# Weight splits held back behind the gated sum and the second norm's sum in a decoder block on one core

## The chip, the cores and the metric

The kernel runs on one core of one Trainium2 chip. The metric is the time of one execution in microseconds (us), lower is better. The core's engines work side by side, each through its own row of instructions in a fixed order, and wait for one another by semaphores: TensorE (PE, matrix products), VectorE (DVE), ScalarE (ACT), GpSimd (POOL) and SyncE (SP), which here issues nearly all transfers from the main memory.

## The reference

One decoder block in float32 with 256 tokens of width 1024. Two attention branches of 8 heads run in parallel, each is multiplied with its own matrix and weighted by a sigmoid gate; the gated sum goes through `w_out`, and a gated feed-forward follows:

```python
br_a = einsum('bse,ed->bsd', o_a, w_branch_moba)
br_b = einsum('bse,ed->bsd', o_b, w_branch_fox)
merged = gates[:, :, 0] * br_a + gates[:, :, 1] * br_b
x = x + einsum('bsd,de->bse', merged, w_out)
h2 = rms_norm(x, ffn_norm_g)              # x * rsqrt(mean(x*x) + eps) * g
u, g = split(einsum('bsd,df->bsf', h2, w_ffn_up), 2)     # 2 x 2816 columns
x = x + einsum('bsf,fd->bsd', silu(conv3(g)) * u, w_ffn_down)
```

The change concerns the stretch from `br_b` to the first columns of the up-projection.

## The kernel before, in words

**Split products.** Every operand of a product is split into a high part (the value copied to PE's shortened float32 format) and a low part (value minus high part). A product is then high x high + high x low + low x high. For each half chunk of weights (128 x 1024), ACT writes the high part (line 134, `whi`) and DVE the low part (line 135, `wlo`). Such a pair is called a weight split here.

**Chunks.** The weights come in chunks of 1 MB (128 x 2048), in a fixed list: the projections, gates (`wg`), four chunks of the two branch matrices (`wb`), four of `w_out` (`wo`), then 22 of the up-projection (`wu`) with 11 of the down-projection (`wd`) among them. SP loads each into one of three buffers `raw`, and a buffer is free again when both halves in it are split. `use(chunk, half)` returns a split half and, unless `state["hold"]` is set, calls `load(upto)`, which issues the loads and splits of all halves up to a number ahead (8 from the last `wb` chunk on). Where `state["behind"]` holds a pair, the splits issued meanwhile are ordered behind these two instructions: the high part on ACT behind the first, the low part on DVE behind the second. Split halves live in six buffers `whi`/`wlo` and, from the last branch chunk on, three out of nine in `V`, `bias` and `qn`, which the attention no longer needs.

**Order.** PE's order is that of the program text. On the other engines a scheduler of the framework sets the order at build time, under the dependencies that the program gives.

**The stretch.** `branch(dh, br)` multiplies attention branch `br` for half `dh` of the columns, multiplies with the gate and, for `br == 1`, adds both branches into `gates[t][dh]` (the tile `lead`; L597 and L599 before). `turn_m(dh)` transposes this gated sum on PE (L607) and writes its high part (ACT, L611) and low part (DVE, L612) into `m2` (the tile `x2`, printed `x`). `rows_of(src, w, h, i, two)` multiplies four of the eight 128-row blocks (`h` says which four, `i` which 128 output columns): for each one pair of products, 128x512 (L641) and 128x256 (L642). The `wo` chunks go in the order (0,0), (1,0), (2,0), (0,1), (1,1), (2,1), (3,0), (3,1), with (chunk, half) in each bracket; the second turn stands within (1,0). When a chunk's columns are complete, `x1_rows(f, ...)` adds the residual (DVE, L651), writes the high and low part of the sum times the norm's gain into `hx` (the tile `pp`; ACT L654, DVE L655), squares it (ACT, L657) and adds up the squares (DVE, L661). `norm2_sum` adds the last two rows of squares (L686), splits the sum (ACT L688, DVE L689), sums over the partitions with two products with a matrix of ones (PE, L692), and computes the norm's factor `rs2` (L695 to L700), which is applied after the up-projection. The up-projection starts with chunks 0 and 1 in the order (0,0), (1,0), (0,1), (1,1), and `norm2_sum` is called within (0,1), after its first four pairs. `up_finish(f)` takes the results out of the banks (ACT L733, DVE L734), applies `rs2` (L735), the convolution and the gate, and writes the activation's parts (ACT L747, DVE L748). `down(p)` multiplies two activations with the p-th `wd` chunk (L765); the first one comes after the products of up chunk 4.

Of the kernel before, what the change touches and what calls it, by code (L numbers as in the profile page):

```python
# [8 lines left out]
F32 = mybir.dt.float32  # L9
F32R = mybir.dt.float32r  # L10
BF16 = mybir.dt.bfloat16
AF = mybir.ActivationFunctionType
ALU = mybir.AluOpType
# [4 lines left out]
P = 128  # L18
S = 256
# [23 lines left out]
def decoder_block(ctx, tc, a, out):  # L43
    nc = tc.nc
# [6 lines left out]
    def T(shape, tag, bufs=1, dt=F32):  # L51
        return sb.tile(shape, dt, tag=tag, bufs=bufs, name=tag)
# [32 lines left out]
    pos = {c: i for i, c in enumerate(chunks)}  # L85
    split = {}
    state = {"next": 0, "raw": None, "ahead": AHEAD, "hold": False, "behind": None}
# [28 lines left out]
    def load(upto):  # L116
        while state["next"] <= min(upto, 2 * len(chunks) - 1):
            i, h = divmod(state["next"], 2)
            state["next"] += 1
            if i < 2:  # L120
                lead(2 * i + h)
                continue
            c = chunks[i]
            if h == 0:
                w = 1024 if i == 2 else 2048
                src = a[c[0]]
                for j in (c[1] - (c[0] == "qkv"), *c[2:]):
                    src = src[j]
                raw = state["raw"] = T([P, 2048], "raw", RB)
                for j in range(2048 // w):  # L130
                    nc.sync.dma_start(raw[:, j * w:(j + 1) * w], src[:, j * w:(j + 1) * w])
            raw = state["raw"][:, h * 1024:(h + 1) * 1024]
            hi, lo = home(2 * i + h)
            whi = nc.scalar.activation(hi, raw, AF.Copy)  # L134
            wlo = nc.vector.tensor_tensor(lo, raw, hi.bitcast(F32), op=ALU.subtract)  # L135
            if state["behind"]:
                for i, j in zip((whi, wlo), state["behind"]):
                    if j:
                        after(i, j)
            split[c, h] = (hi, lo, whi)  # L140

    def use(c, h):
        if not state["hold"]:
            load(2 * pos[c] + h + state["ahead"])
        return split.pop((c, h))[:2]
# [60 lines left out]
    def pairs(ap):  # L206
        return ap.rearrange("p (a t) -> p t a", a=2)
# [256 lines left out]
    gates = [[lt[:, 4 * t + g, S:] for g in range(4)] for t in range(NT)]  # L464
# [26 lines left out]
    def banks():  # L491
        return [bank() for _ in range(NT)]
# [53 lines left out]
    two = [first_half(1, pair) for pair in range(2)]  # L546
# [4 lines left out]
    two = [banks() for _ in range(2)]  # L551
# [22 lines left out]
    high = values(1, (2, 3))  # L574
    for g in range(4):
        last = gate_sigmoid(g, copied if g == 3 else last_exp[0])
# [5 lines left out]
    m2 = T([P, KT, 2, 2, P], "x2", 1, F32R)  # L582
    def branch(dh, br):
        ps_ = banks()
        for hh in range(2):
            wh, wl = use(("wb", 2 * dh + br), hh)
            state["behind"] = None
            for k2 in range(2):
                k = 2 * hh + k2
                oh, ol = (x[:, 4 * br + k] for x in heads)  # L590
                rh, rl = (pairs(w[:, k2 * 512:(k2 + 1) * 512]) for w in (wh, wl))
                for i, (lhs, rhs) in enumerate(((oh, rh), (oh, rl), (ol, rh))):
                    for t in range(NT):
                        nc.tensor.matmul(ps_[t], lhs[:, t * P:(t + 1) * P], rhs, start=(k == 0 and i == 0), stop=(k == 3 and i == 2))  # L594
        for t in range(NT):
            m = gates[t][2 * br + dh]
            nc.vector.tensor_tensor(m, ps_[t], m, op=ALU.mult)  # L597
            if br == 1:
                nc.vector.tensor_tensor(gates[t][dh], gates[t][dh], m, op=ALU.add)  # L599

    def turn_m(dh):
        two = banks()
        for t in range(NT):
            for n in range(4):
                c = slice((2 * n + t) * HD, (2 * n + t + 1) * HD)
                for r, (rows, eye) in enumerate(parts):
                    nc.tensor.transpose(two[r][:, c], gates[t][dh][rows, n * P:(n + 1) * P], eye)  # L607
        for r in range(2):
            src = two[r].rearrange("p (n t c) -> p n t c", n=4, t=NT)
            high, low = (m2[:, 4 * dh:4 * dh + 4, :, l, r * HD:(r + 1) * HD] for l in range(2))  # L610
            nc.scalar.activation(high, src, AF.Copy)  # L611
            nc.vector.tensor_tensor(low, src, high.bitcast(F32), op=ALU.subtract)  # L612

    branch(0, 0)
    branch(0, 1)
    branch(1, 0)
    turn_m(0)
    state["base"], state["ahead"] = 2 * pos["wb", 3], AHEAD + 3
    branch(1, 1)


    hx = T([P, KT, 2, 2, P], "pp", 1, F32R)
# [8 lines left out]
    def wide(ps_):  # L631
        return ps_.rearrange("p (j c) -> p j c", j=2)

    def rows_of(src, w, h, i, two):
        wh, wl = w
        for k4 in range(4):
            k = 4 * h + k4
            c = slice(k4 * 256 + i * P, k4 * 256 + (i + 1) * P)
            both = src[:, k].rearrange("p a l t -> p (l t) a")
            high = src[:, k, :, 0].rearrange("p a t -> p t a")  # L640
            nc.tensor.matmul(two[i], wh[:, c], both, start=(k == 0), stop=False)  # L641
            nc.tensor.matmul(two[i][:, 0:S], wl[:, c], high, start=False, stop=(k == KT - 1))  # L642

    sums = []

    def x1_rows(f, two):
        for i in range(2):
            d = 2 * f + i
            x, g = xT[:, d], col(C_G2 + d)
            for part in (1, 0):  # L650
                nc.vector.tensor_tensor(halves(xT[:, d:d + 1]), apart(two[i][:, part * S:(part + 1) * S], 1), halves(xT[:, d:d + 1]), op=ALU.add)  # L651
            high, low = (hx[:, d, :, l] for l in range(2))
            x = x.rearrange("p (a t) -> p a t", a=2)
            nc.scalar.activation(high, x, AF.Copy, scale=g)  # L654
            nc.vector.scalar_tensor_tensor(low, x, g, high.bitcast(F32), op0=ALU.mult, op1=ALU.subtract)  # L655
        sq = T([P, 2, S], "lows", 2) if f == 0 else T([P, 2, S], "sq", 2)
        nc.scalar.activation(sq, xT[:, 2 * f:2 * f + 2], AF.Square)  # L657
        if f == 0:
            sums.append(sq)
        else:  # L660
            nc.vector.tensor_tensor(sums[0], sums[0], sq, op=ALU.add)  # L661

    tw = [banks() for _ in range(2)]
    for f in range(2):
        w = use(("wo", f), 0)
        for i in range(2):
            rows_of(m2, w, 0, i, tw[f])
            if f == 1 and i == 0:
                turn_m(1)
    tw.append(banks())  # L670
    for f, h in ((2, 0), (0, 1), (1, 1), (2, 1)):
        w = use(("wo", f), h)
        for i in range(2):
            rows_of(m2, w, h, i, tw[f])
        if h:
            x1_rows(f, tw[f])
    tw.append(banks())
    for h in range(2):
        w = use(("wo", 3), h)
        for i in range(2):  # L680
            rows_of(m2, w, h, i, tw[3])
    x1_rows(3, tw[3])

    def norm2_sum():
        ss = sums[0]
        nc.vector.tensor_tensor(ss[:, 0], ss[:, 0], ss[:, 1], op=ALU.add)  # L686
        two = T([P, 2, S], "lows", 2, F32R)
        nc.scalar.activation(two[:, 0], ss[:, 0], AF.Copy)  # L688
        nc.vector.tensor_tensor(two[:, 1], ss[:, 0], two[:, 0].bitcast(F32), op=ALU.subtract)  # L689
        o = bank()  # L690
        for l in range(2):
            nc.tensor.matmul(o[:, 0:S], ones, two[:, l], start=(l == 0), stop=(l == 1))  # L692
        w = T([P, 3, S], "s", 4)
        v, y, t = w[:, 0], w[:, 1], w[:, 2]
        nc.vector.tensor_scalar(v, o[:, 0:S], 1.0 / D, EPS, op0=ALU.mult, op1=ALU.add)  # L695
        nc.scalar.activation(t, v, AF.Ln)
        nc.scalar.activation(y, t, AF.Exp, scale=-0.5)
        nc.vector.scalar_tensor_tensor(t, v, -0.5, y, op0=ALU.mult, op1=ALU.mult)
        nc.vector.tensor_tensor(t, t, y, op=ALU.mult)
        nc.vector.scalar_tensor_tensor(rs2, t, 1.5, y, op0=ALU.add, op1=ALU.mult)  # L700
# [15 lines left out]
    def up_half(f, h, two):  # L716
        w = use(("wu", f), h)
        for i in range(2):
            rows_of(hx, w, h, i, two)
            if f == i == 0 and h == 1:  # L720
                norm2_sum()

    def up_products(f):
        two = banks()
# [77 lines left out]
    for h in range(2):  # L802
        for f in range(2):
            up_half(f, h, first[f])
    for f in range(NF):
        low = up_finish(f, first[f] if f < 2 else up_products(f))
        if f % 2 == 0 and f >= 4:
            down(f // 2 - 2)
        if TURN <= f < TURN + KT:
            turn_x(f - TURN, low)  # L810
        if f == TURN + KT:
            spread_x()
# [73 lines left out]
```

## Time and profile before

| what | value |
|---|---|
| time of the kernel, median of 3 runs | 353.95 us (353.56 to 354.65) |
| the profiled execution: its time, its span | 357.12 us, 355.3 us |
| busy: PE, weight loads, DVE, ACT | 98%, 86%, 83%, 62% of the span |
| transfers | 70.1 MB, 197 GB/s in the mean |
| mean granted TensorE clock | 0.990 |

A row of the timeline gives the start in us, the duration in us, the engine, the line and the operation, the tile written and the tiles read, and in square brackets the idle time ahead of it with what ended it. Neighbouring rows can overlap a little, since the instructions of an engine are pipelined. A row of windows gives busy microseconds of PE, weight loads (PEld), DVE, ACT and POOL in that stretch, with counts in brackets, then the granted clock, the share of the transfer engines and GB/s. A list of waits has the waiting instruction, what it waited for, the total in us, how often, and the longest.

### The profile page before, as it was taken

How to read it: one execution, taken by the hardware profiler on the slowest of the kernel's cores; microseconds unless marked ns; L12 is line 12 of the kernel's file. 1: busy time of each engine (PE TensorE's matmuls, PEld its weight loads, DVE VectorE, ACT ScalarE, POOL GpSimd, SP SyncE). 2: the span in 40 equal slices, each digit the busy share in tenths (PEclk: the TensorE clock that was granted, in tenths of full speed). 3: DMA queues.
4: the chain of work that ended last, by engine and by line, in shares of the span. 5: the costliest groups of instructions: out<-in, count | busy, mean ns of one | idle time of the engine just before them, and what ended most of it. 6: DMA issues, size and time to landing. Idle time of an engine off the chain costs nothing.

```text
span 355.3 us, 5446 instructions
## 1 busy us (share of the span) xinstructions
PE 347.5 (98%) x2047; PEld 304.1 (86%) x2047; DVE 295.9 (83%) x556; ACT 221.8 (62%) x385; POOL 1.3 (0%) x8
## 2 busy tenths in 40 slices
PE   8999999999999999999969999999999999999996
PEld 4878888888888888889959989899898989989885
DVE  5899997999689588998977997888879888887833
ACT  4868654958299394747556876556665775575420
POOL 0000000000000000000000000000000000000000
PEclk9999999999999999999978999999999999999999
DMA  7987863675612736494553555564663654546003
GB/s 275 400 331 255 289 235 129 220 259 216 225 72 70 287 118 239 129 368 171 179 220 118 194 177 222 221 209 162 238 218 138 236 218 167 223 105 237 0 2 118
DMA packets 14410, 70.10 MB, mean 197 GB/s; under 512 B 1832, under 2 KB 5040, under 8 KB 6960
## 3 DMA queue, kind: packets, MB, share of 16 engines
q1 hardware_dynamic: 13184, 68.69, 53.3%
q10 hardware_dynamic: 1200, 1.06, 0.9%
q8 instruction: 16, 0.26, 0.3%
q14 instruction: 10, 0.08, 0.1%
HBM read 67.64 MB, written 1.06 MB: 193 GB/s over the span
## 4 chain that ended last, share of the span: by engine, by line
PE 85%; DVE 6%; DMA 6%; ACT 1%; issue 1%; ACTq 0%; DVEq 0%
PE bank L246 30%; PE bank L641 21%; PE bank L765 16%; PE bank L642 10%; DMA raw<-in_wu 3%; DVE wlo L135 2%; PE bank L594 2%; PE bank L457 2%; DMA raw<-in_wo 1%; DVE lead L651 1%; PE bank L443 1%; DMA g<-in_g 1%; ACT whi L134 1%; DVE pp L655 1%; PE bank L290 1%
## 5 line engine op out<-in xcount | busy, mean ns | idle before, releaser
L135 DVE TENSOR_TENSOR wlo<-raw,whi 128x1024 fp32r<-128x1024 f32 x94 | 113.9, 1220 | 12.0 <-ACT whi L134 11.6
L134 ACT ACTIVATE whi<-raw 128x1024 fp32r<-128x1024 f32 x94 | 98.2, 1056 | 30.9 <-PE bank L641 10.7
L246 PE MATMUL bank<-whi,x 128*128 128x512 f32 x320 | 83.7, 381 | 0.2 <-DVE x L161 0.2
L641 PE MATMUL bank<-pp,whi 128*128 128x512 f32 x232 | 79.0, 391 | 0.0
L246 PEld LDWEIGHTS bank<-whi,x 128*128 128x128 f32 x320 | 59.9, 189 | 10.1 <-ACT whi L102 0.8
L642 PE MATMUL bank<-pp,wlo 128*128 128x256 f32 x232 | 64.4, 278 | 0.0
L641 PEld LDWEIGHTS bank<-pp,whi 128*128 128x128 f32 x232 | 45.1, 195 | 6.7
L246 PE MATMUL bank<-wlo,x 128*128 128x512 f32 x160 | 48.0, 381 | 0.0
L642 PEld LDWEIGHTS bank<-pp,wlo 128*128 128x128 f32 x232 | 45.6, 197 | 0.2
L246 PEld LDWEIGHTS bank<-wlo,x 128*128 128x128 f32 x160 | 29.9, 189 | 5.2 <-DVE wlo L103 0.8
L765 PE MATMUL bank<-whi,qT 128*128 128x512 f32 (+1 forms) x92 | 27.8, 370 | 0.0
L734 DVE TENSOR_TENSOR sq<-bank,lows 128x256 f32<-128x256 f32 x44 | 18.1, 416 | 10.0 <-ACT lows L733 10.0
L733 ACT ACTIVATE lows<-bank 128x256 f32<-128x256 f32 x44 | 16.1, 370 | 9.4 <-PE bank L642 8.7
L742 ACT ACTIVATE s<-s 128x256 f32<-128x256 f32 x22 | 9.1, 414 | 16.5 <-DVE s L741 16.5
L739 ACT ACTIVATE s<-sq,sm 128x256 f32<-128x256 f32 x22 | 13.1, 595 | 9.9 <-DVE sq L735 9.9
L765 PEld LDWEIGHTS bank<-whi,qT 128*128 128x128 f32 x92 | 17.2, 189 | 2.3
L641 PE MATMUL bank<-pp,bias 128*128 128x512 f32 x56 | 18.7, 382 | 0.0
L765 PE MATMUL bank<-wlo,qT 128*128 128x512 f32 (+1 forms) x46 | 17.0, 370 | 0.0
L594 PE MATMUL bank<-whi,pp 128*128 128x512 f32 x64 | 17.0, 382 | 0.0
L735 DVE TENSOR_TENSOR sq<-sq,rsB 128x512 f32<-128x512 f32 x22 | 15.2, 690 | 0.6
L642 PE MATMUL bank<-pp,bias 128*128 128x256 f32 x56 | 15.3, 273 | 0.0
L424 ACT ACTIVATE s<-s,nm 128x128 f32<-128x128 f32 (+1 forms) x32 | 14.1, 452 | 0.0
(181 smaller groups left out, 563.6 us busy)
## 6 DMA issues: line engine op xcount, KB each, us to landing
raw<-in_wu SPq DMA_DIRECT2D x22, 1024.0 KB, 4.9
raw<-in_wd SPq DMA_DIRECT2D x11, 1024.0 KB, 4.8
raw<-in_qkv SPq DMA_DIRECT2D x9, 1024.0 KB, 5.4
raw<-in_wg SPq DMA_DIRECT2D x8, 1024.0 KB, 4.9
raw<-in_wb SPq DMA_DIRECT2D x4, 1024.0 KB, 5.3
raw<-in_wo SPq DMA_DIRECT2D x4, 1024.0 KB, 4.8
lead<-in_lead SPq DMA_DIRECT2D x8, 384.0 KB, 6.0
raw<-in_qkv SPq DMA_DIRECT2D x2, 512.0 KB, 8.2
```

The source lines that it names most:

```text
L134: whi = nc.scalar.activation(hi, raw, AF.Copy)
L135: wlo = nc.vector.tensor_tensor(lo, raw, hi.bitcast(F32), op=ALU.subtract)
L246: nc.tensor.matmul(pt[t], lhs[:, k, t * P:(t + 1) * P], rhs, start=(k == 0 and i == 0), stop=(k == KT - 1 and i == 2))
L424: last_exp[:] = [nc.scalar.activation(s[:, j, c], s[:, j, c], AF.Exp, scale=-1.0, bias=nm[:, j, i:i + 1], accum_out=l[:, j, i:i + 1])]
L594: nc.tensor.matmul(ps_[t], lhs[:, t * P:(t + 1) * P], rhs, start=(k == 0 and i == 0), stop=(k == 3 and i == 2))
L641: nc.tensor.matmul(two[i], wh[:, c], both, start=(k == 0), stop=False)
L642: nc.tensor.matmul(two[i][:, 0:S], wl[:, c], high, start=False, stop=(k == KT - 1))
L733: nc.scalar.activation(lows[:, i:i + 1].rearrange("p b (a t) -> p b a t", a=2), apart(two[i][:, S:2 * S], 1), AF.Copy)
L734: nc.vector.tensor_tensor(halves(ev[:, i:i + 1]), apart(two[i][:, 0:S], 1), halves(lows[:, i:i + 1]), op=ALU.add)
L735: nc.vector.tensor_tensor(ev, ev, rs2[:, None, :].to_broadcast([P, 2, S]), op=ALU.mult)
L739: nc.scalar.activation(cv, g, AF.Identity, scale=col(C_CW + 2 * NF + f), bias=col(C_CB + f))
L765: nc.tensor.matmul(o, lhs, rhs, start=(first and i == 0), stop=(end and i == 2))
```

## The change

Three things are done. In the last branch the second half's `use` is held (`state["hold"]`), so that the splits it would have issued come after its additions, in two portions: behind the last addition (`merged`), and behind the low parts of the second turn. The second turn itself stands two pairs of products later. From chunk 3 of `wo` on, the splits are held again until the second norm's sum has been split: the sum is taken up within `x1_rows` (for chunk 3 in two half-width additions), its high and low part are written there, and the held low parts are ordered behind the last of these (`summed`). The ones products stand after the whole of (0,1) instead of after its first four pairs. Only low parts are ordered so; the high parts on ACT are not. The work itself is the same but for the shape of the additions. The names of lines move: L597 becomes L598, L599 L600, L607 L609, L611 and L612 become L613 and L614, L641 and L642 L644 and L645, L651 L654, L654 and L655 become L657 and L658, L657 L660, L692 L710, L695 L713, L733 and L734 become L751 and L752, L748 L766.

```diff
@@ branch
             state["behind"] = None
+            state["hold"] = dh == br == 1
...
             if br == 1:
-                nc.vector.tensor_tensor(gates[t][dh], gates[t][dh], m, op=ALU.add)
+                done = nc.vector.tensor_tensor(gates[t][dh], gates[t][dh], m, op=ALU.add)
+        return done if br else None
@@ turn_m
-            nc.vector.tensor_tensor(low, src, high.bitcast(F32), op=ALU.subtract)
+            last = nc.vector.tensor_tensor(low, src, high.bitcast(F32), op=ALU.subtract)
+        return last
...
-    branch(1, 1)
+    merged = branch(1, 1)
@@ rows_of
-    def rows_of(src, w, h, i, two):
+    def rows_of(src, w, h, i, two, quarters=range(4)):
...
-        for k4 in range(4):
+        for k4 in quarters:
@@ x1_rows
             sums.append(sq)
-        else:
-            nc.vector.tensor_tensor(sums[0], sums[0], sq, op=ALU.add)
+            return
+        ss = sums[0]
+        if f < 3:
+            nc.vector.tensor_tensor(ss, ss, sq, op=ALU.add)
+        if f == 2:
+            nc.vector.tensor_tensor(ss[:, 0], ss[:, 0], ss[:, 1], op=ALU.add)
+        if f == 3:
+            for i in range(2):
+                nc.vector.tensor_tensor(ss[:, 0], ss[:, 0], sq[:, i], op=ALU.add)
+            two = T([P, 2, S], "lows", 2, F32R)
+            nc.scalar.activation(two[:, 0], ss[:, 0], AF.Copy)
+            sums.append(two)
+            return nc.vector.tensor_tensor(two[:, 1], ss[:, 0], two[:, 0].bitcast(F32), op=ALU.subtract)
@@ w_out
-    for f in range(2):
-        w = use(("wo", f), 0)
-        for i in range(2):
-            rows_of(m2, w, 0, i, tw[f])
-            if f == 1 and i == 0:
-                turn_m(1)
+    w = use(("wo", 0), 0)
+    for i in range(2):
+        rows_of(m2, w, 0, i, tw[0])
+    state["hold"], state["behind"] = False, (None, merged)
+    load(2 * pos["wo", 0] + state["ahead"])
+    state["hold"] = True
+    w = use(("wo", 1), 0)
+    rows_of(m2, w, 0, 0, tw[1])
+    rows_of(m2, w, 0, 1, tw[1], range(2))
+    state["hold"], state["behind"] = False, (None, turn_m(1))
+    load(2 * pos["wo", 1] + state["ahead"])
+    state["behind"] = None
+    rows_of(m2, w, 0, 1, tw[1], range(2, 4))
...
+    state["hold"] = True
     tw.append(banks())
...
-    x1_rows(3, tw[3])
+    summed = x1_rows(3, tw[3])
@@ norm2_sum
-        ss = sums[0]
-        nc.vector.tensor_tensor(ss[:, 0], ss[:, 0], ss[:, 1], op=ALU.add)
-        two = T([P, 2, S], "lows", 2, F32R)
-        nc.scalar.activation(two[:, 0], ss[:, 0], AF.Copy)
-        nc.vector.tensor_tensor(two[:, 1], ss[:, 0], two[:, 0].bitcast(F32), op=ALU.subtract)
+        two = sums[1]
@@ up_half
-            if f == i == 0 and h == 1:
-                norm2_sum()
+        if f == 0 and h == 1:
+            norm2_sum()
@@ first up chunks
             up_half(f, h, first[f])
+            if h == f == 0:
+                state["hold"], state["behind"] = False, (None, summed)
+                load(2 * pos["wu", 0] + state["ahead"])
+                state["behind"] = None
```

What the scheduler makes of it on DVE at the second turn, first before and then now (numbers tell buffers of one name apart; `qn`, `wlo` rows are low parts of weights, `lead` the gated sum):

```order
L135 TENSOR_TENSOR qn_1682<-raw_1679,qn_1681 128x1024
L135 TENSOR_TENSOR wlo_1698<-raw_1679,whi_1697 128x1024
L597 TENSOR_TENSOR lead_78<-bank_1665,lead_78 128x512
L597 TENSOR_TENSOR lead_78<-bank_1666,lead_78 128x512
L599 TENSOR_TENSOR lead_78<-lead_78 128x512 x2
L135 TENSOR_TENSOR wlo_1728<-raw_1725,whi_1727 128x1024
```

```order
L135 TENSOR_TENSOR qn_1682<-raw_1679,qn_1681 128x1024
L598 TENSOR_TENSOR lead_78<-bank_1665,lead_78 128x512
L598 TENSOR_TENSOR lead_78<-bank_1666,lead_78 128x512
L600 TENSOR_TENSOR lead_78<-lead_78 128x512 x2
L135 TENSOR_TENSOR wlo_1738<-raw_1679,whi_1737 128x1024
L135 TENSOR_TENSOR wlo_1744<-raw_1741,whi_1743 128x1024
```

One weight split (the second half of the last `wo` chunk, out of `raw_1679`) moved from ahead of the gated sum's products and additions to behind them.

On DVE at the second norm's sum, before (from the split of up chunk 3's second half to the sum's low part):

```order
L135 TENSOR_TENSOR qn_1930<-raw_1908,qn_1929 128x1024
L651 TENSOR_TENSOR lead_78<-bank_1906,lead_78 128x256
L651 TENSOR_TENSOR lead_78<-bank_1907,lead_78 128x256
L651 TENSOR_TENSOR lead_78<-bank_1906,lead_78 128x256
L651 TENSOR_TENSOR lead_78<-bank_1907,lead_78 128x256
L135 TENSOR_TENSOR wlo_1967<-raw_1964,whi_1966 128x1024
L655 SCALAR_TENSOR_TENSOR pp_1717<-lead_78,sm_79,pp_1717 128x2x128 x2
L661 TENSOR_TENSOR lows_1847<-lows_1847,sq_1957 128x512
L135 TENSOR_TENSOR wlo_1987<-raw_1964,whi_1986 128x1024
L135 TENSOR_TENSOR wlo_1993<-raw_1990,whi_1992 128x1024
L686 TENSOR_TENSOR lows_1847<-lows_1847 128x256
L689 TENSOR_TENSOR lows_2021<-lows_1847,lows_2021 128x256
```

and now (up to the first instruction that reads the ones products, L713):

```order
L668 TENSOR_TENSOR lows_1847<-lows_1847 128x256
L654 TENSOR_TENSOR lead_78<-bank_1908,lead_78 128x256 x2
L658 SCALAR_TENSOR_TENSOR pp_1713<-lead_78,sm_79,pp_1713 128x2x128 x2
L671 TENSOR_TENSOR lows_1847<-lows_1847,sq_1949 128x256 x2
L675 TENSOR_TENSOR lows_1953<-lows_1847,lows_1953 128x256
L135 TENSOR_TENSOR bias_1978<-raw_1976,bias_1978 128x1024
L135 TENSOR_TENSOR qn_1982<-raw_1976,qn_1981 128x1024
L135 TENSOR_TENSOR wlo_1988<-raw_1985,whi_1987 128x1024
L135 TENSOR_TENSOR wlo_1992<-raw_1985,whi_1991 128x1024
L135 TENSOR_TENSOR wlo_1998<-raw_1995,whi_1997 128x1024
L713 TENSOR_SCALAR s_2036<-bank_2033 128x256
```

Five splits (`bias`, `qn` and three `wlo`: up chunks 3 and 4 and the first half of down chunk 0; the `bias` one stood a little ahead of the rows shown) moved from between and ahead of the sum's additions to behind its low part, and now stand ahead of L713.

On PE at the ones products, before and now:

```order
L641 MATMUL bank_1960<-pp_1717,whi_1747 128x512
L642 MATMUL bank_1960<-pp_1717,wlo_1748 128x256
L692 MATMUL bank_2024<-lows_2021,ones_1719 128x256 x2
L641 MATMUL bank_1961<-pp_1717,whi_1747 128x512
L642 MATMUL bank_1961<-pp_1717,wlo_1748 128x256
```

```order
L644 MATMUL bank_1957<-pp_1713,whi_1781 128x512
L645 MATMUL bank_1957<-pp_1713,wlo_1782 128x256
L710 MATMUL bank_2033<-lows_1953,ones_1715 128x256 x2
L644 MATMUL bank_1958<-pp_1713,whi_1797 128x512
L645 MATMUL bank_1958<-pp_1713,wlo_1798 128x256
```

Before, the ones products stand between the two column blocks of half (0,1), which read `whi_1747`; now they stand after both, ahead of half (1,1), which reads `whi_1797`.

## The prediction

> **What bounds the kernel now.** I read the page's busy shares and slices first, then the list of waits for TensorE (PE) alone, then the timeline around each wait it names.
>
> ```profile
> PE 347.5 (98%) x2047; PEld 304.1 (86%) x2047; DVE 295.9 (83%) x556; ACT 221.8 (62%) x385; POOL 1.3 (0%) x8
> ...
> PEclk9999999999999999999978999999999999999999
> ```
>
> PE is the bound: it is busy nearly all the time, so only what it waits for, or runs slowly through, can be won. The granted clock dips once, in slices 21 and 22 (177.7 to 195.4 us). The list of PE's waits over the whole span has four rows (in total, times, longest), two of them from the first 5 us; the other two are:
>
> ```profile
> PE bank L692 <- ACT lows L688: 3.1, 1, 3.1
> ...
> PE bank L607 <- DVE lead L599: 0.2, 1, 0.2
> ```
>
> These are two places that the change touches: the ones products (L692) and the second turn of the gated sum (L607). PE's timeline at the ones products, and the windows (us, then busy times, near the end of the row the granted clock):
>
> ```profile
> 179.03 0.40 PE L641 MATMUL bank<-pp,whi 128*128 128x512 f32 x1
> 179.27 0.27 PE L642 MATMUL bank<-pp,wlo 128*128 128x256 f32 x1
> 182.60 1.04 PE L692 MATMUL bank<-lows,ones 128*128 128x256 f32 x2 [3.06 <-ACT lows L688]
> 183.44 0.63 PE L641 MATMUL bank<-pp,whi 128*128 128x512 f32 x1
> ...
> 188.78 0.27 PE L642 MATMUL bank<-pp,wlo 128*128 128x256 f32 x1
> 188.89 0.38 PE L641 MATMUL bank<-pp,whi 128*128 128x512 f32 x1
> ```
>
> ```profile
> 181.70:181.80 0.10, 0.00 (x0) 0.00 (x0) 0.10 (x2) 0.00 (x0) 0.00 (x0) 0.61 1.17 164
> 183.44:188.56 5.12, 5.12 (x18) 4.39 (x17) 3.47 (x7) 2.21 (x5) 0.00 (x0) 0.50 0.25 104
> 188.56:193.80 5.24, 5.24 (x34) 4.82 (x33) 3.89 (x8) 3.40 (x6) 0.00 (x0) 1.00 0.58 200
> ```
>
> So the wait costs twice. PE has nothing from 179.37 (one step of 0.11 after the last start; its pipeline runs out at 179.54) to 182.60, and in that gap the clock falls to 0.50, at about 181.72 (0.61 is the mean of the tenth of a microsecond that begins at 181.70). The next 5.12 us hold eight pairs of products (0.64 each). At full clock 16 pairs take 5.24, so a pair is 0.328. Why the ones products wait is in the rows of VectorE (DVE) and ScalarE (ACT):
>
> ```profile
> 172.29 1.22 DVE L135 TENSOR_TENSOR bias<-raw,bias 128x1024 fp32r<-128x1024 f32 x1
> ...
> 174.43 1.22 DVE L135 TENSOR_TENSOR qn<-raw,qn 128x1024 fp32r<-128x1024 f32 x1
> 175.56 1.41 DVE L651 TENSOR_TENSOR lead<-bank,lead 128x256 f32<-128x256 f32 x4
> 176.89 1.21 DVE L135 TENSOR_TENSOR wlo<-raw,whi 128x1024 fp32r<-128x1024 f32 x1
> ...
> 178.81 0.68 DVE L661 TENSOR_TENSOR lows<-lows,sq 128x512 f32<-128x512 f32 x1
> 179.41 2.35 DVE L135 TENSOR_TENSOR wlo<-raw,whi 128x1024 fp32r<-128x1024 f32 x2
> 181.69 0.41 DVE L686 TENSOR_TENSOR lows<-lows 128x256 f32<-128x256 f32 x1
> 182.58 0.42 DVE L689 TENSOR_TENSOR lows<-lows 128x256 fp32r<-128x256 f32 x1 [0.48 <-ACT lows L688]
> ```
>
> ```profile
> 177.49 0.62 ACT L657 ACTIVATE sq<-lead 128x512 f32<-128x512 f32 x1
> 178.00 2.00 ACT L134 ACTIVATE whi<-raw 128x1024 fp32r<-128x1024 f32 x2
> 182.13 0.42 ACT L688 ACTIVATE lows<-lows 128x256 fp32r<-128x256 f32 x1 [2.13 <-DVE lows L686]
> ```
>
> DVE is full here, and five weight splits (bias, qn and three wlo, 1.14 us from start to start) stand among the additions that feed L689, which ends at 183.00. None of the five is needed soon: they are the up-projection's fourth and fifth chunk and the first down chunk.
>
> **The change, part by part.** *Splits behind the second norm's sum.* The five low parts now follow L675, the old L689. Taking 5 x 1.14 = 5.7 out of DVE's row puts its end at 177.3 at the earliest. Walking the new rows with ACT in the line gives 177.9: the last two L654 end near 175.0, the scaled copy (L657) near 175.5, the square (L660) near 176.0, two half-width additions near 176.7, then the ACT split that stands ahead of L673 ends at 177.05, and L673 and L675 take 0.42 each. The additions themselves cost the same within 0.1 (two 512-wide and three 256-wide ahead of the low part, for three and one).
>
> *Ones products later.* They move behind four more pairs, 1.31 us. With the turn's gain below PE arrives at 179.37 + 1.31 - 0.60 = 180.08, some 2.2 after its input is ready. The wait goes: 183.44 - 179.37 = 4.07, less the two ones products. No row shows these unstalled. The nearest, L642 with the same 128x256, steps on after 0.11 (188.78 to 188.89), so 0.22 for two; the stalled start-to-next of 0.84 is the other end. I take 0.22, since it is the same shape at full clock: gain 3.85 (3.23 at least).
>
> *The clock.* With PE busy on both sides no gap is left, and the eight pairs take 2.62 in place of 5.12: gain 2.50. It could be 0 in an execution that lacked the dip.
>
> *Turn and the splits behind the gated sum's additions.*
>
> ```profile
> 143.97 0.59 PE L594 MATMUL bank<-whi,pp 128*128 128x512 f32 x2
> 144.49 0.71 PE L607 MATMUL bank<-cst,lead 64*128 64x64 f32 x16
> 145.13 0.70 PE L594 MATMUL bank<-whi,pp 128*128 128x512 f32 x2
> ...
> 154.24 0.27 PE L642 MATMUL bank<-x,wlo 128*128 128x256 f32 x1
> 154.68 1.06 PE L607 MATMUL bank<-cst,lead 64*128 64x64 f32 x16 [0.17 <-DVE lead L599]
> 155.68 0.48 PE L641 MATMUL bank<-x,whi 128*128 128x512 f32 x1
> ```
>
> ```profile
> 151.62 1.21 DVE L135 TENSOR_TENSOR wlo<-raw,whi 128x1024 fp32r<-128x1024 f32 x1
> 152.75 1.28 DVE L597 TENSOR_TENSOR lead<-bank,lead 128x512 f32<-128x512 f32 x2
> 153.95 1.28 DVE L599 TENSOR_TENSOR lead<-lead 128x512 f32<-128x512 f32 x2
> ```
>
> From one step after the last product's start (0.11 for 256 wide, 0.22 for 512) to the next product, the second turn takes PE 155.68 - 154.35 = 1.33; the first one, whose input was ready, 145.13 - 144.40 = 0.73. Its second half waits for the second L599 (155.23). One split moved behind brings that to 154.1, and two pairs moved ahead let PE come at 155.0. Gain 0.60, at worst 0.17 (the wait shown), at best no more.
>
> What the held split pays: that low part ends at 155.3 instead of 152.83. It frees the buffer of the third up chunk's transfer, issued here at 152.86; now 155.3, 2.5 later.
>
> ```profile
> 152.86 0.33 SPq L131 DMA_DIRECT2D raw<-in_wu  x1
> ...
> 160.52 1.08 ACT L134 ACTIVATE V<-raw 128x1024 fp32r<-128x1024 f32 x1 [1.42 <-DMA raw<-in_wu]
> 161.63 1.23 DVE L135 TENSOR_TENSOR V<-raw,V 128x1024 fp32r<-128x1024 f32 x1 [1.27 <-ACT V L134]
> 162.78 1.67 DVE L651 TENSOR_TENSOR lead<-bank,lead 128x256 f32<-128x256 f32 x4
> raw<-in_wu SPq DMA_DIRECT2D x22, 1024.0 KB, 4.9
> ```
>
> That split (V) stands ahead of L651, the start of the whole chain to the sum. Issue to landing was 7.6 there, with two chunks ahead of it in the engines; the median is 4.9. From 155.3 that makes 160.2: no later. I cost it at nothing, with 0 and 2.5 as ends for the chain, of which the margin of 2.2 absorbs all but 0.3.
>
> *What queues behind the sum.* The five splits now run from 177.9 to about 183.6, ahead of L713 and the evacuations. On SyncE's queue the sixth up chunk's transfer, issued here when the qn split ends at 175.65, goes out at about 180.2, and lands at 185.1. PE wants it only after the first down products, near 204 in the new time. The nearest consumer is those products themselves:
>
> ```profile
> 196.64 0.41 DVE L748 TENSOR_TENSOR qT<-s,qT 128x256 fp32r<-128x256 f32 x1
> ...
> 205.59 0.38 PE L765 MATMUL bank<-whi,qT 128*128 128x512 f32 x1
> ```
>
> They would start at 205.59 - 6.95 = 198.6. Behind the five splits, DVE's new rows hold four more (4.6), two 512-wide steps (0.6 each) and 16 small ones (0.41 as L748) up to the first activation's low part: 183.6 + 12.3 = 195.9. Cover 2.7; cost 0.
>
> Sum: 3.85 + 2.50 + 0.60 = 6.95. The profiled execution took 357.12 (span 355.3), so 350.17 under the profile. The runs' median is 353.95, 3.17 below it; I take the whole loss to be in the median too, and get **347.0**.
>
> [...] PE had nothing in hand for 3.06 us (the row of L692), the clock fell before that wait was over, and it stayed at half until about 188.5, 6.8 in all. [...]
>
> **The rivals.** *No dip in the timed runs.* The profiled execution is 3.17 above the median and the dip is worth 2.50, so the dip may belong to the profiled execution alone. Then only 3.85 + 0.60 is won: 353.95 - 4.45 = 349.5. Against it: the gap exceeds three microseconds in every execution, since its cause is a fixed order. The three runs, within 1.1, could be all with a dip or all without.
>
> *The sum is still late* (the change then does half of what it says). If the third up chunk lands a full transfer later, 4.9 after 160.5, the chain ends at 182.8 and PE waits 2.7. A dip of up to 2.5 may remain: 353.95 - 0.60 - 1.15 gives 352.2 with it, 349.7 without. For it: V is directly ahead of L651. Against it: the two chunks ahead will have passed sooner.
>
> *Slower: the five splits push the first activation behind the first down products.* Place: L766, ahead of the products that started at 205.59. To lose over 0.3% (1.06, about what a measurement here can tell from no change) PE must wait 6.95 + 1.06 = 8.0 there, the low part must come at 206.6, 10.7 later than summed. That is nearly twice the held work (5.7). At the deciding point the time is 355.0; I give 355.5.
>
> **How the numbers follow.** The full gain: 0.62, 347.0, by itself 345.8 to 348.2. No dip: 0.20, 349.5. Sum still late: 0.10, 349.7 to 352.2. Activation late, slower: 0.04, 355.5. Gains and new waits cancelling within 0.3%: 0.04. Range 345.7 to 350.4: its top takes in the no-dip case and the ones products at 0.84, its bottom a dip longer by 1.3 in the timed runs than here; it leaves out the activation and cancelling cases and most of the late sum, under 0.2. Faster 0.62 + 0.20 + 0.10 = 0.92, same 0.04, slower 0.04.
>
> **What would show it.** In the changed profile PE's waits should lack the ones products and the turn, the clock be 9 in every slice, the second turn take 0.7 of PE, the ones products start near 180.1, L675 end near 178, and V's split start no later than 161. A row "L710 <- L673 or L675" in PE's waits falsifies the walk; a clock dip without one, my reading of the dip; a new PE wait at the down products (old L765), the cover of 2.7. A profiled gain near 7 with a timed gain near 4.5 would show the no-dip rival.

## The result and the profile after

The changed kernel takes 350.13 us (median of 4 runs, 349.78 to 350.19) against 354.24 for the kernel before in the same session: a ratio of 0.9884, with a 95% interval of 0.9865 to 0.9902. It is faster by 4.1 us. The forecast was 347.0 with a range of 345.7 to 350.4: the direction was right and the time lies inside the range, near its top. The profiled execution took 350.19, where the prediction's sum for it was 350.17. The medians here and below leave out two disturbed executions, one of 604.26 in the changed kernel run again and one of 1291.5 in the first part alone with its gap filled.

PE's list of waits has one row left, from the start of the kernel, and the page's row of granted clocks has no dip:

```profile
PE bank L170 <- PEq L901: 0.8, 1, 0.8
```

```profile
PEclk9999999999999999999999999999999999999999
```

PE's timeline at the second turn (L609) and at the ones products (L710) shows both without idle time ahead of them. From one step after the last product to the next one the turn takes 155.72 - 154.99 = 0.73, and the ones products 180.31 - 180.06 = 0.25:

```profile
154.88 0.27 PE L645 MATMUL bank<-x,wlo 128*128 128x256 f32 x1
155.08 0.71 PE L609 MATMUL bank<-cst,lead 64*128 64x64 f32 x16
155.72 0.48 PE L644 MATMUL bank<-x,whi 128*128 128x512 f32 x1
...
179.95 0.27 PE L645 MATMUL bank<-pp,wlo 128*128 128x256 f32 x1
180.06 0.41 PE L710 MATMUL bank<-lows,ones 128*128 128x256 f32 x2
180.31 0.38 PE L644 MATMUL bank<-pp,whi 128*128 128x512 f32 x1
```

VectorE's (DVE's) rows show the five held splits behind the sum's low part (L675), which ends at 179.81, only 0.25 ahead of PE. The chain to it started late, with the V split:

```profile
163.39 1.23 DVE L135 TENSOR_TENSOR V<-raw,V 128x1024 fp32r<-128x1024 f32 x1 [2.26 <-ACT V L134]
...
179.39 0.42 DVE L675 TENSOR_TENSOR lows<-lows 128x256 fp32r<-128x256 f32 x1 [0.48 <-ACT lows L673]
179.74 1.22 DVE L135 TENSOR_TENSOR bias<-raw,bias 128x1024 fp32r<-128x1024 f32 x1
180.87 1.22 DVE L135 TENSOR_TENSOR qn<-raw,qn 128x1024 fp32r<-128x1024 f32 x1
182.01 3.49 DVE L135 TENSOR_TENSOR wlo<-raw,whi 128x1024 fp32r<-128x1024 f32 x3
185.41 0.41 DVE L713 TENSOR_SCALAR s<-bank 128x256 f32<-128x256 f32 x1
```

ScalarE's high part for that split waited for the third up chunk, which SyncE's queue issued at 155.89:

```profile
155.89 0.33 SPq L131 DMA_DIRECT2D raw<-in_wu  x1
```

```profile
162.30 1.06 ACT L134 ACTIVATE V<-raw 128x1024 fp32r<-128x1024 f32 x1 [2.80 <-DMA raw<-in_wu]
```

Further on, the first activation's low part ends at 197.17, and the first down products start at 198.65 without a wait:

```profile
196.76 0.41 DVE L766 TENSOR_TENSOR qT<-s,qT 128x256 fp32r<-128x256 f32 x1
```

```profile
198.65 0.38 PE L783 MATMUL bank<-whi,qT 128*128 128x512 f32 x1
```

So the profiles differ by 6.93 (357.12 and 350.19) and the medians by 4.1. The experiments ask where the other 2.8 went, and which of the edits carries the gain.

### The profile page after: what moved, and what is told of

It reads as the page before. It is cut to its first block, busy times and chain, and to the rows that moved or that the text cites. A ratio compares the mean times of both kernels' runs of the same rounds, so it can differ in the third digit from the quotient of the medians.

```text
span 348.4 us, 5439 instructions
## 1 busy us (share of the span) xinstructions
PE 344.2 (99%) x2047; PEld 302.8 (87%) x2047; DVE 294.8 (85%) x557; ACT 219.7 (63%) x385; POOL 1.3 (0%) x8
## 4 chain that ended last, share of the span: by engine, by line
PE 99%; DVE 0%; issue 0%
PE bank L246 30%; PE bank L644 26%; PE bank L783 16%; PE bank L645 13%; PE bank L595 6%; PE bank L457 2%; PE bank L170 1%; PE bank L443 1%; PE bank L290 1%; PE bank L393 1%; PE bank L400 0%; PE bank L406 0%; PE bank L609 0%; PE bank L320 0%; PE bank L358 0%; DVE s L816 0%
## 5 line engine op out<-in xcount | busy, mean ns | idle before, releaser
L644 PE MATMUL bank<-pp,whi 128*128 128x512 f32 x232 | 76.6, 382 | 0.0
L645 PE MATMUL bank<-pp,wlo 128*128 128x256 f32 x232 | 63.2, 273 | 0.0
L644 PEld LDWEIGHTS bank<-pp,whi 128*128 128x128 f32 x232 | 43.8, 189 | 6.1
L645 PEld LDWEIGHTS bank<-pp,wlo 128*128 128x128 f32 x232 | 44.5, 192 | 0.2
L752 DVE TENSOR_TENSOR sq<-bank,lows 128x256 f32<-128x256 f32 x44 | 18.0, 415 | 7.4 <-ACT lows L751 7.3
L644 PE MATMUL bank<-pp,bias 128*128 128x512 f32 x56 | 18.7, 382 | 0.0
L751 ACT ACTIVATE lows<-bank 128x256 f32<-128x256 f32 x44 | 15.6, 367 | 1.9 <-PE bank L645 1.9
L645 PE MATMUL bank<-pp,bias 128*128 128x256 f32 x56 | 15.3, 273 | 0.0
```

The lines of the kernel that those rows point to most:

```text
L751: nc.scalar.activation(lows[:, i:i + 1].rearrange("p b (a t) -> p b a t", a=2), apart(two[i][:, S:2 * S], 1), AF.Copy)
L752: nc.vector.tensor_tensor(halves(ev[:, i:i + 1]), apart(two[i][:, 0:S], 1), halves(lows[:, i:i + 1]), op=ALU.add)
```

## The experiments

All times are medians of several runs, 4 to 12 of each kernel; the kernel before, run beside them on the same chips, had 354.62, 354.59 and 354.57 in the three groups (59 runs in all). The theory at their start was that the clock dip behind PE's gap comes in some executions only.

| kernel | us | ratio to before (95% interval) | clock in its profile |
|---|---|---|---|
| before again | 354.57 | 1.0000 (0.9986 to 1.0015) | 0.995 |
| first part alone (turn) | 356.74 | 1.0059 (1.0038 to 1.0081) | 0.990 |
| second part alone (sum) | 350.16 | 0.9881 (0.9862 to 0.9901) | 1.000 |
| ones products later, alone | 352.18 | 0.9948 (0.9919 to 0.9976) | 1.000 |
| before, gap filled | 353.12 | 0.9967 (0.9946 to 0.9988) | 0.999 |
| before, gap longer | 358.83 | 1.0125 (1.0095 to 1.0154) | 0.990 |
| changed, again | 349.89 | 0.9880 (0.9849 to 0.9910) | 0.998 |
| changed, ones products early | 349.96 | 0.9878 (0.9850 to 0.9905) | 1.000 |
| changed, second hold undone | 352.96 | 0.9949 (0.9926 to 0.9971) | 1.000 |
| changed, first hold undone | 349.93 | 0.9866 (0.9845 to 0.9886) | 0.998 |
| first part alone, gap filled | 353.79 | 0.9978 (0.9951 to 1.0004) | 1.000 |

**The kernel before, again** (no edit).

> The kernel before, unchanged, to see how often the clock dips behind the gap of 3.1 us ahead of the ones products. Theory A (the dip comes in some executions only, since the gap is about as long as what the clock needs to fall): among the runs some show a mean granted clock near 0.99 and take about 357, the others a clock near 1.00 and about 354.2; the first kind is the rarer one. Rival B (every execution has the dip, and the profiled one is longer for another reason): all runs show 0.99 and about 354, and the profile again 357.

Its 12 runs lie between 353.45 and 355.38, its profiled run at 355.38 with a clock of 0.995. That profile is neither of the two kinds: the dip is there, but half as long. PE's rows and the windows around the ones products:

```profile
178.98 0.27 PE L642 MATMUL bank<-pp,wlo 128*128 128x256 f32 x1
181.86 0.85 PE L692 MATMUL bank<-lows,ones 128*128 128x256 f32 x2 [2.60 <-ACT lows L688]
182.54 0.38 PE L641 MATMUL bank<-pp,whi 128*128 128x512 f32 x1
```

```profile
181.20:181.86 0.66, 0.00 (x1) 0.00 (x1) 0.18 (x2) 0.42 (x1) 0.00 (x0) 1.00 0.33 124
182.80:182.90 0.10, 0.10 (x3) 0.10 (x2) 0.10 (x1) 0.00 (x0) 0.00 (x0) 0.90 1.93 819
182.94:186.35 3.41, 3.41 (x12) 2.96 (x12) 2.30 (x6) 2.16 (x4) 0.00 (x0) 0.51 0.29 120
186.20:186.30 0.10, 0.10 (x2) 0.10 (x1) 0.10 (x1) 0.00 (x0) 0.00 (x0) 0.53 0.00 0
```

Here PE resumes at full clock, the clock falls only at 182.88 and returns at 186.29, 3.41 later; in the execution recorded first it was low for 6.8. The wait is shorter too, 2.60 against 3.06. So the dip's length and the wait both change from execution to execution.

How often each kind comes is on record too, as every run has its mean granted clock. A low clock of 3.41 lowers the mean of such a span by about 0.005, one of 6.8 by about 0.010 (an estimate: half the length over some 353). The 59 runs of the kernel before fall into just these three groups:

| mean granted clock | runs | time, us | median, us |
|---|---|---|---|
| 0.999 or 1.000 (no dip) | 17 | 352.79 to 353.91 | 353.20 |
| 0.994 or 0.995 (the short dip) | 39 | 354.22 to 356.75 | 354.68 |
| 0.990 (the long dip) | 3 | 356.85 to 357.96 | 357.73 |

Of the 12 runs of this experiment two are of the first kind, ten of the second, none of the third. So theory A was right that some runs have no dip, but most have a short one, and the execution recorded first, with 357.12 and 0.990, is of the rarest kind. That the gap is about as long as what the clock needs to fall was the author's estimate: in that execution it fell 2.18 after PE's last product had ended (181.72 and 179.54), within a wait of 3.06, and in the profile here it was still at 1.00 when a wait of 2.60 ended (181.86). The short dip costs 354.68 - 353.20 = 1.48.

**The gap filled.** This takes the clock away from the wait:

```diff
         o = bank()
+        for _ in range(22):
+            nc.tensor.matmul(o[:, S:2 * S], warm[:, 0:P], warm[:, 0:S], start=True, stop=True)
         for l in range(2):
             nc.tensor.matmul(o[:, 0:S], ones, two[:, l], start=(l == 0), stop=(l == 1))
```

> The kernel before with 22 products of constants (128x256, bf16) ahead of the ones products, into the unused half of their bank: they fill some 2.4 us of PE's gap and change nothing that is computed. The wait for the sum stays, the clock has no idle time to fall in. Theory A, revised by the runs so far (the length of the dip changes from run to run, about 1.0 us of it in the timed runs' median): clock 1.00 in the profile, 354.6 - 1.0 = 353.6. Rival A0 (the timed runs lack the dip): 354.6. Rival B (all have the whole dip): 352.1.

```profile
179.07 2.64 PE L692 MATMUL bank<-const-bfloat16-1.0 128*128 128x256 bf16 x22
181.46 0.73 PE L694 MATMUL bank<-lows,ones 128*128 128x256 f32 x2
182.03 0.38 PE L641 MATMUL bank<-pp,whi 128*128 128x512 f32 x1
```

The sum is as late as ever, and PE's useful work still waits for it, but PE is busy meanwhile: 353.12, with a clock of 0.999. Against 354.59 that is 1.47 faster, the dip's share in the median of the kernel before, and it is the time that the kernel before has in its runs without a dip (353.20). What is left to the changed kernel, 353.12 - 350.13 = 2.99, should be the wait and the turn. The rows give nearly that: here 182.03 - 179.07 - 0.25 = 2.71 of wait, and at the turn 155.38 - 154.21 = 1.17 against 0.73, so 0.44.

```profile
154.10 0.27 PE L642 MATMUL bank<-x,wlo 128*128 128x256 f32 x1
154.39 1.06 PE L607 MATMUL bank<-cst,lead 64*128 64x64 f32 x16
155.38 0.48 PE L641 MATMUL bank<-x,whi 128*128 128x512 f32 x1
```

**The gap longer.** The opposite: ten copies between the sum's last addition and its split.

```diff
         nc.vector.tensor_tensor(ss[:, 0], ss[:, 0], ss[:, 1], op=ALU.add)
+        for _ in range(5):
+            nc.vector.tensor_copy(ss[:, 1], ss[:, 0])
+            nc.vector.tensor_copy(ss[:, 0], ss[:, 1])
```

> The kernel before with ten copies of 128x256 within the second norm's sum, ahead of its split, which leave its value as it is: about 3.7 us more of gap for PE. With a gap near 7 us the dip is in every run and long. Theory A revised: 354.6 + 3.7 + (2.6 - 1.0) = 359.9, clock 0.98 to 0.99. Rival A0: 354.6 + 3.7 + 2.6 = 360.9. Rival B: 358.3.

The copies took 0.33 from start to start (the first and the last row of L688 and L689: 181.04 and 184.00), so 3.29 in all, not 3.7. The time is 358.83, 4.24 more. The 0.95 above the copies agrees with a dip that is now long in every run, as all six have a clock of 0.990: 2.5 - 1.47 = 1.03 was to come. PE's wait in the profile is 5.4, and the means of two windows put the dip from 183.40 to 190.22:

```profile
PE bank L695 <- ACT lows L691: 5.4, 1, 5.4
```

```profile
182.00:184.00 2.00, 0.00 (x0) 0.00 (x0) 1.77 (x7) 0.00 (x0) 0.00 (x0) 0.85 0.78 328
190.00:191.00 1.00, 1.00 (x7) 0.95 (x6) 0.87 (x2) 0.31 (x1) 0.00 (x0) 0.89 0.00 0
```

**The second part alone** (the hold in the last branch and the second turn's place as before).

> Only the second part: splits held behind the second norm's sum, the sum taken up within x1_rows, the ones products four pairs later; the turn and its split as before. Theory A: no wait at the ones products, no dip, the turn's 0.60 stays lost: 350.13 + 0.6 = 350.7, and the low part of the sum is ready near 178, over 2 us before PE, as the V split is not delayed. Rival B (the turn's part is worth nothing or harms): 350.1 or less.

350.16, as fast as the whole change. The profile has no wait at the ones products, and the sum's low part ends at 177.12, with PE there at 180.32:

```profile
176.69 0.43 DVE L674 TENSOR_TENSOR lows<-lows 128x256 fp32r<-128x256 f32 x1 [0.48 <-ACT lows L672]
```

From the first `w_out` product to the first that reads V, PE takes 6.54 here and 6.07 in the changed kernel's second profile, and the last products start 0.54 apart (344.94 and 344.40). So the turn's gain is in the profiles; in the medians (350.16 against 350.13 and 349.89) it isn't clear of the noise, with runs that spread by 0.4 to 0.7.

**The first part alone** (the sum and the ones products as before).

> Only the first part of the change: the split held behind the gated sum's additions, the two portions, the turn two pairs later; the second norm's sum and the ones products as before. Theory A (parts are not additive, as the ones products wait for VectorE, whose chain starts with the V split and its transfer): PE's 0.60 at the turn is given back at the ones products, whose wait grows by 0.6, and the later transfer of the third up chunk (V split 1.8 later in the changed kernel) lengthens it by up to 1.8 more: 354.2 to 356.0 without a dip, and, as the gap is then 3.7 to 5.5 us, the dip in most runs, 2.5 more: 356.5 to 358.5. Rival B (parts add): 0.6 faster, 353.6.

356.74: slower than before by 2.1, though the turn takes PE 0.73, where it took 1.17 to 1.35 in the profiles with the old turn. The profile shows why: the wait, and a dip of 6.8 again, from 181.14 to 187.96 by the means of its first and last window.

```profile
PE bank L702 <- ACT lows L698: 3.1, 1, 3.1
```

```profile
181.00:181.69 0.69, 0.00 (x0) 0.00 (x0) 0.21 (x2) 0.42 (x1) 0.00 (x0) 0.60 0.15 24
182.53:187.65 5.12, 5.12 (x18) 4.39 (x17) 3.47 (x7) 2.21 (x5) 0.00 (x0) 0.50 0.28 115
187.00:188.00 1.00, 1.00 (x5) 0.90 (x4) 0.77 (x2) 0.11 (x1) 0.00 (x0) 0.52 0.00 0
```

Four of its six runs have a clock of 0.990, the other two 0.995, where the kernel before had 0.990 in 3 of 59.

The later transfer is not in this profile (V split at 160.99). To tell the dip from it, the same kernel with 26 products in the gap:

> The kernel with the first part alone (356.74 against 354.6), with 26 products of constants ahead of the ones products, into the unused half of their bank, some 2.8 us of PE's gap. If its loss is the dip, now in every run, and the turn's gain is given back at the ones products: 2.6 less, 354.1, with a clock of 1.00. If the loss is the later transfer: 356 or more.

353.79, with a clock of 1.00: 2.95 of the time was the dip, more than the whole loss. PE's gain at the turn lengthened a gap whose end VectorE sets (a wait of 3.06, against 2.60 in the kernel before run again, with the V split at 160.99 and 161.31), and with the longer gap the long dip came more often (four of six runs against 3 of 59). What stays open is why this is still 0.67 above the kernel before with its gap filled (353.12): in the two profiles the V split starts 0.32 later (161.03 and 160.71), and the rest no run separates.

**The ones products later, alone** (`norm2_sum` called after both column blocks of half (0,1)).

> Only the place of the ones products: four pairs later, all else as before. Theory A: their input still comes at about 183.0, PE arrives 1.31 later, the wait falls from 3.1 to about 1.8, and a gap of 1.8 brings no dip in any run: 354.24 - 1.31 = 352.9, the profile near 352.9 with a clock of 1.00. Rival B (the dip follows any wait there): profile near 355.5, clock 0.99.

352.18: 2.4 faster where the move itself is worth 1.31. The rest, 1.1, is dip that a shorter gap mostly lacks: the profile waits 0.8 and has a clock of 1.00, and so have nine other runs (0.999 or 1.000). But two of the twelve, at 355.04 and 355.63, have 0.995, so "no dip in any run" was too strong.

**The second hold undone** (the second `state["hold"] = True` and the `load` behind `summed` left out; the sum still taken up within `x1_rows`).

> The changed kernel without the second hold: the sum is taken up within x1_rows and the ones products stand later, but the five splits are issued as before; on VectorE they fall between the sum's additions again. If the hold is what carries the gain: the sum's low part ends near 182.5, PE waits some 2.4, and the time is that of the ones products moved alone (352.2) or up to 1 more with dips. If the new shape of the sum carries it: 350.1.

352.96. The splits fall among the additions again, and PE waits at three places, for the scaled rows and for both parts of the sum, 2.4 in all (the row of 0.8 is the one from the start of the kernel):

```profile
PE bank L644 <- DVE pp L658: 1.4, 1, 1.4
PE bank L170 <- PEq L896: 0.8, 1, 0.8
PE bank L709 <- DVE lows L675: 0.6, 1, 0.6
PE bank L709 <- ACT lows L673: 0.4, 1, 0.4
```

```profile
181.43 1.22 DVE L135 TENSOR_TENSOR wlo<-raw,whi 128x1024 fp32r<-128x1024 f32 x1
182.56 0.41 DVE L675 TENSOR_TENSOR lows<-lows 128x256 fp32r<-128x256 f32 x1
```

So the hold carries the last 2.8, and the new shape of the sum does not. The rows of VectorE say the same without the chance of when the V split starts: from that start to the end of the sum's low part it is 20.60 here (162.37 to 182.97), 20.96 to 21.37 in the six profiles with the old sum and no copies added, and 16.28 to 16.43 in the five with the second hold.

**The changed kernel again, and with the ones products early** (called where they stood before).

> The changed kernel again, for the spread of its runs and for where the V split falls in another execution. Expected 350.1, no dip. If the held split really delays the third up chunk, the V split starts again near 163.4 (DVE), and the sum's low part ends within half a microsecond of PE's arrival; if that was chance, V starts near 161 and the low part ends 2 us or more ahead of PE.

> The changed kernel with the ones products back after the first four pairs of half (0,1), all other edits kept (VectorE's order is the same). It tells what the later place is worth once the splits are held. If the sum's low part ends as in the profile of the changed kernel (179.8), PE, there at 178.75, waits 1.1: 351.2. If it ends as with the sum part alone (177.1), no wait: 350.1. By my prediction's walk (177.9): no wait.

349.89 and 349.96. The V split starts at 162.22 in the first profile, 160.66 in the second, with one and the same order on VectorE; the transfer was issued at 154.78 and 154.60, and ScalarE's part started at 161.11 and 159.57. Both expectations had a share. The first hold does delay the transfer: it goes out at 154.6 to 155.9 in the six profiles with that hold and at 152.3 to 152.9 in the seven without. But the V split starts at 160.66 to 163.39 with it and at 160.03 to 161.63 without, so how much of the delay reaches VectorE differs between executions, and no run shows why. With the splits held the sum's low part ended at 177.09 in the second, 1.3 ahead of PE at 178.42, so in these runs the later place of the ones products is worth nothing on top of the hold. It is a margin for executions such as the first recorded one of the changed kernel, where the low part came at 179.81.

```profile
176.67 0.42 DVE L675 TENSOR_TENSOR lows<-lows 128x256 fp32r<-128x256 f32 x1 [0.48 <-ACT lows L673]
```

```profile
178.42 0.41 PE L710 MATMUL bank<-lows,ones 128*128 128x256 f32 x2
```

**The first hold undone** (the split ahead of the gated sum again, the turn still two pairs later).

> The changed kernel without the first hold: the turn still stands two pairs later, but the split of the last w_out chunk's second half comes ahead of the gated sum again, so that the third up chunk's transfer goes out some 2.3 earlier. If the hold is what gives the turn its gain: PE waits up to 0.2 at the turn and the time is 350.1 to 350.4. The V split should start no later than 161.6, as in all runs without the held split so far, and the sum's low part should end 2.5 ahead of PE.

349.93 (349.80 to 350.05), no worse than the change, and PE does not wait at the turn (0.71 there, no row in its list). The V split starts earliest of all, and the sum's low part is ready 3.2 ahead of PE (176.45 and 179.69):

```profile
160.03 1.23 DVE L135 TENSOR_TENSOR V<-raw,V 128x1024 fp32r<-128x1024 f32 x1 [0.16 <-ACT V L134]
```

So at the turn the two pairs do the work; the hold there buys nothing that these runs can measure and costs margin. The difference of 0.2 to the changed kernel is within the spread of the runs, so this version isn't shown to be faster.

## Why the prediction was right, and where a step failed

*The bound and the two waits.* Right. Both rows of PE's waits are gone, and nothing took their place.

*Splits behind the sum.* The direction was right and the hold is what carries it. The walk put the low part's end at 177.9, that is 16.3 behind the old start of the V split (161.63); measured were 16.28 to 16.43. The ends themselves, 179.81, 178.65, 177.12, 177.09 and 176.45, differ because the V split's start does.

*Ones products later.* 0.25 for two unstalled ones products was forecast as 0.22, PE's arrival at 180.06 as 180.08. Here too the sum against the profile was right.

*The late transfer, costed at nothing.* The step was wrong, and the cover held: the transfer was issued 0.6 later than forecast and took 6.4 from issue to use in the first profile of the changed kernel, where I took the median 4.9, and the V split came 1.8 later than before. The margin of 2.2 fell to 0.25, and that it was just enough there was luck.

*The cover at the down products.* 2.7 was forecast, 1.5 measured in the first profile, 2.4 in the second (196.01 and 198.36). No wait.

*The sum.* Against the profiled execution it was 6.95, measured 6.93. The step that failed is the last: "I take the whole loss to be in the median too". The terms came from one execution that had the longest wait and dip among the profiles of the kernel before, and its time of 3.17 above the median said so; 3 of 59 runs are of its kind. In the median the clock's term of 2.50 is 1.47 (filled gap). The ones products' 3.85 is 2.71 and the turn's 0.60 is 0.44 in the profile with the filled gap, whose time, 353.20, is near its median. (In the kernel before run again, profiled at 355.38, the 3.85 is 182.54 - 179.09 - 0.25 = 3.20.) Most of the 1.14 by which the wait's term was too large goes with the V split, which started at 161.63 in the execution recorded first and at 160.71 with the gap filled. With these sizes the sum is 4.62, and from 354.59 the forecast would have been 350.0, close to the 350.13. The base was a little off as well: the three runs had 353.95, the 59 have about 354.6.

*The rivals.* The no-dip rival's gain of 4.45 is near the 4.1 measured, but by coincidence: it had no dip and a whole wait, where the runs had a part of each. The forecast's own case alone, 345.8 to 348.2, missed, and the stated range held the result only because its top was set to take in this rival, with the ones products at 0.84. The argument against the rival, that the gap exceeds three microseconds in every execution because the order is fixed, was wrong: with the same order the wait was 2.60 in the kernel before run again. The late sum did not come, though it came within 0.25. The slower case did not come with the whole change; the first part alone is slower, in a way that I did not list: PE came earlier to a gap that VectorE ends, waited 3.06 there, and four of its six runs had the long dip.

## What to carry to other kernels

Before a sum over waits is set against a median, compare the profiled execution's own time with the median: an excess as large as one of the terms can mean that the term is not in every run. Here the mean clock of each run told how often the dip comes, and filling the gap with products of constants priced it apart from the wait. PE's wait of 2.60 to 3.06 us cost more than its length here, as the clock fell in 42 of 59 runs (1.47 in the median, by the gap filled), and a gain ahead of it made the kernel slower (356.74 against 354.62). When one engine's row is full, look at which of its instructions nobody needs soon, and hold those: here, with five weight splits held behind one sum, neither the turn's part nor the later place of the ones products changed the median any more. A kernel with that hold alone was not run.

## What the runs showed of the hardware

Two lengths of the low clock were seen: 3.41 (182.88 to 186.29 in the kernel before, run again), and 6.82 or 6.83 in three profiles (181.72 to 188.55 in the first recorded execution, 181.14 to 187.96 with the first part alone, 183.40 to 190.22 with the gap longer). In these three the clock fell to 0.50 while PE waited, 2.18, 2.51 and 4.01 after its last product had ended (179.54, 178.63 and 179.39), and PE took up its work at half the clock. In the kernel before, run again, the clock was still at 1.00 when the wait of 2.60 ended at 181.86, and fell 1.02 later, with PE at work. In the profiles of the ones products moved alone (a wait of 0.8) and of the gap filled the clock had no dip (means of 1.00 and 0.999). No run shows what sets the moment at which the clock falls, or which of the two lengths comes.

I had not expected the granted clock to cost such different amounts with one and the same code: eight pairs of products took 5.12 in one execution (0.64 each), and in another the first pair behind the gap still ran at full clock (182.54 to 182.87, 0.33).
